# Output projection of an attention layer by token halves, with the values of a head in two runs and a third bank for transposes

## The chip, the cores and the metric

The kernel runs on one core of a Trainium2 chip. A core has TensorE (matmuls, with results in the banks of PSUM), VectorE, ScalarE and GpSimd, which here hardly works, and SyncE (SP), which issues the transfers from HBM. The profile calls them PE, DVE, ACT, POOL and SP. What is measured is the device time of one launch in microseconds; the time of a kernel is the median of several runs.

## The reference, cut to what matters

Two layers work on 512 latent tokens with 1024 features and 256 context tokens. Each layer is a feed-forward block, a mixer and a second feed-forward block; the mixer of layer 0 is a gated convolution, that of layer 1 is attention with 8 heads of queries, two of keys and values and a head size of 128. All data are fp32. The change touches the attention, the residual behind it and the start of the norm of the last feed-forward block:

```python
def gqa_block(q, k, v):
    s = jnp.einsum('bqkgd,bskd->bkgqs', q, k).astype(jnp.float32) * (HEAD_DIM ** -0.5)
    p = jax.nn.softmax(s, axis=-1).astype(v.dtype)
    return jnp.einsum('bkgqs,bskd->bqkgd', p, v)
...
    y_lat = o_l @ w_o                              # attention_mixer, o_l: (1, 512, 8 * 128)
...
        x_lat = x_lat + m_lat[:, 1, 2] * y_lat     # reference, layer 1
        h = norm_modulate(x_lat, norm_g[i, 2], m_lat[:, 2, 0], m_lat[:, 2, 1])
        x_lat = x_lat + MACARON_WEIGHT * m_lat[:, 2, 2] * swiglu(h, ffn_w_in[i, 1], ffn_w_out[i, 1])
```

Keys and values cover 768 tokens, context and latent; in layer 1 only the 512 latent tokens have queries and an output. `norm_modulate` needs the sum of the squares of all 1024 features of a token, so the norm of a token can begin only when its whole projection is done.

## The kernel before

**Products.** Features lie on the partitions (8 chunks m of 128), tokens in the columns. Every fp32 operand is split in two fp32r parts, high and low: ScalarE copies the high part (L184), VectorE subtracts it and writes the low part (L185). A product is then three matmuls, high by high, high by low and low by high (`mm3`, L805 to L807). A split of a weight tile of 128x512 is thus one instruction on each of the two engines, and so is every operand that TensorE is to read.

**Weights.** `w_list` lists all weight tiles in the order of their use, each with a place and, if its place comes free late, an event that must have been passed before the split may be written. `w_fill(k)` issues up to k further splits from this list at the point of the program where it stands, `w_get(k)` takes the next tile, and fills as far as k allows before, `w_done()` gives back the places of the tiles taken (`GRANULES` is their number). SP issues the raw transfers well ahead, in the order of the list.

**Order.** TensorE and SP execute in program order. The instructions of ScalarE and VectorE are put in order by a list scheduler when the kernel is built, which may pull a split or a subtract ahead of what stands before it in the program; between `in_order()` and `free_order()` they stay as written.

**Scores.** 8 heads by 4 blocks of 128 tokens are 32 blocks, n = 0 to 31. `scores` makes 6 matmuls into a tile of ps_C (two banks; there are two such tiles), then the max (VectorE, L1435), its product with the scale of the queries (L1436), the exponential with its sum on ScalarE (L1438), the reciprocal of the sum (L1439), and the scaling of the row, on ScalarE in odd blocks (L1441), on VectorE in even ones (L1443). `turn` transposes the 768 columns of the block in two half-turns of three (L1454), each into one of the two T banks, and splits each. `values` multiplies two blocks at once with the values: 18 matmuls of 256 columns into ps_O, whose result is split into o. In the loop the scores run two blocks ahead, and the values of a pair run behind the turn of the next block: scores(n+2), turn(n), then for even n values. A pair below is two scores, two turns, one run of values.

Ahead of the loop stand the value projections, `value_chunk` 0 to 5 (24 matmuls into ps_B, results read out by L1386 and L1387), and between them the norms of the last queries; chunks 4 and 5 stand behind the first two scores.

**Output projection.** While heads 4 to 7 run, a filler (`out_steps`, L856 on) does the part of heads 0 to 3: per m one group of 12 matmuls (4 heads, three parts) with all 512 columns into the bank of ps_A, which is the bank S, and an eviction that adds the group to x (L871). Behind the loop `out_close` does heads 4 to 7, first for token half one (columns 0 to 255), then for half two, 12 matmuls of 256 columns per m and half, evictions at L941. Its weight tiles 0 to 5 are held in slots that come free with the event "heads", at the end of the loop, so they are split there; the two others lie in homes wo0 and wo1.

**The norm of the last block.** For a token half: "squares" per m (ScalarE L594, VectorE L595), "parts" splits the sum (th on ScalarE L614, tl on VectorE L615), "root" adds over the partitions with two matmuls (L621, L622) and takes the root, and "normed", "modulated" and "parted" make the operands of the last feed-forward block. In `out_close` root of half one stands behind the second group of the second pass; that of half two stands in the opening of the feed-forward block. That block opens with steps of 24 matmuls (four times 6, 256 columns each), and `OPENING` says behind which six of them each part of the norm is put: key (2, 1) is step 2, behind its second six.

Of the kernel before, what the change touches and what calls it, by code (L numbers as in the profile page):

```python
# [41 lines left out]
HALF = D // 2  # L42
CONV_PARTS = (4, 4)
# [30 lines left out]
HELD_AFTER_HEADS = ((4, 5), (8, 9))  # L74
# [51 lines left out]
def backbone(ctx: ExitStack, tc: tile.TileContext, a: dict, out: bass.AP):  # L126
# [108 lines left out]
    def place(n, where, k):  # L235
# [5 lines left out]
        elif where[0] == "home":  # L241
            t = homes[where[1]](f"w{n}")
        else:
# [148 lines left out]

    def w_list():
# [573 lines left out]

    OPENING = {(0, 0): [("squares", 1, [7])], (0, 2): [("parts", 1)], (2, 0): [("root", 1)],
# [7 lines left out]
    def opening_hooks(op, count):  # L976
# [6 lines left out]
        hooks = {at: do(items) for at, items in OPENING.items()}  # L983
# [273 lines left out]
    def attention(gp, i, s, after):  # L1257
# [8 lines left out]
        for u in range(2):  # L1266
            homes["o", u] = lambda n, u=u: gp.tile([P, 2, D // 2], F32R, name=n, tag=f"wo{u}")
        part_tiles[:] = (gp, "th"), (gp, "tl")

        with psum(B=2, S=1, Q=1), ExitStack() as core:  # L1270
# [102 lines left out]
            def value_chunk(sc):  # L1373
                post = heads.pop(0)() if heads else None
                p = ptile("B", (P, 2, 256))[:, 0, :]
                ts = slice(sc * P, (sc + 1) * P)
                for k in range(KC):
                    if post and k == KC // 2:
                        post()
                    wvh, wvl = (t[:, 2 * (k % 2) : 2 * (k % 2) + 2, :] for t in wv[k // 2])  # L1380
# [3 lines left out]
                for g in range(KVH):  # L1384
                    pg = p[:, g * HD : (g + 1) * HD]
                    act.activation(vh[g][:, sc, :], pg, AF.Copy)  # L1386
                    dve.tensor_tensor(out=vl[g][:, sc, :], in0=pg, in1=vh[g][:, sc, :].bitcast(F32), op=ALU.subtract)  # L1387
# [14 lines left out]
            dve.tensor_scalar_mul(nrq, nrq, -isq)  # L1402

# [13 lines left out]
            st = {}  # L1417
# [28 lines left out]
            def turn(h, blk, pr):  # L1446
# [4 lines left out]
                for c0 in (0, 3):  # L1451
                    pt = ptile("T", (P, 4, P))[:, :3, :]
# [6 lines left out]
            def values(h, half, ph, pl):  # L1459
                g = h // 4  # L1460
                if half == 0:
                    st["po"] = ptile("O", (P, 2, 2 * P))
                    if h % 4 == 0:
                        st["o"] = o_tiles(g)
                p = st["po"][:, half, :]
                for c in range(6):
                    mm3(p, vh[g][:, c, :], vl[g][:, c, :], ph[:, c, :], pl[:, c, :], c == 0, c == 5)
                hs = slice(half * 2 * P, (half + 1) * 2 * P)
                oh, ol = st["o"]
                split(oh[h % 4][:, hs], ol[h % 4][:, hs], p)  # L1470

# [314 lines left out]
```

## Time and profile before

| | us |
|---|---|
| median of 3 runs | 2434.13 |
| lowest and highest | 2431.51, 2436.7 |
| the profiled execution, whole | 2436.43 |
| its span in the trace | 2434.7 |

| stretch of the span, us | length | TensorE busy | VectorE busy | ScalarE busy |
|---|---|---|---|---|
| 0 to 1850, all up to the attention | 1850 | 1832.2 | 1536.4 | 810.0 |
| 1850 to 1914, keys, queries, values | 64 | 62.68 | 54.21 | 42.86 |
| 1914 to 2053, scores and output projection | 139 | 130.22 | 107.23 | 97.13 |
| 2053 to 2110, second pass and opening | 57 | 54.55 | 43.37 | 35.67 |
| 2110 to 2434.7, last feed-forward block | 324.7 | 315.68 | 249.66 | 163.47 |

The busy time of TensorE counts a matmul from its start to its modelled end, also when it runs at a lower clock; so a stretch in which TensorE is busy throughout can still lose time, and the granted clock has to be read beside it. In rows of the profile L12 is line 12 of the kernel, `ps_T<-ident,pr` is an instruction that writes ps_T and reads ident and pr, `x3` is a count, and `[0.34 <-DVE p L185]` says that the engine stood for 0.34 us ahead of the row and what released it. In rows of the timeline the first number is the time from the start of the span and the second a duration, both in us.

### The profile page before, as it was taken

The page shows a single profiled execution, that of the slowest core. Times are in us where ns is not written, and L with a number is a line of the kernel's source. Part 1 is how long each engine was busy: PE and PEld are TensorE (multiplying, and loading weights), DVE is VectorE, ACT ScalarE, POOL GpSimd, SP SyncE. Part 2 cuts the span into 40 slices and gives each one's busy share as a digit, 9 for nine tenths or more (in the row PEclk, how much of TensorE's full clock was granted, in tenths as well). Part 3 has the DMA queues.
Part 4 walks back from the last instruction along what each step waited for, and adds up shares of the span by engine and source line. Part 5 has one row for each costly group of instructions (what it writes and reads, how often), then busy time and mean ns, then how long its engine had stood idle before and what let it go on. Part 6 is the DMA issues. An engine that isn't in the chain of part 4 may idle for free.

```text
span 2434.7 us, 37332 instructions
## 1 busy us (share of the span) xinstructions
PE 2395.3 (98%) x14316; PEld 2265.7 (93%) x14316; DVE 1990.9 (82%) x3979; ACT 1149.1 (47%) x2174; POOL 1.2 (0%) x8
## 2 busy tenths in 40 slices
PE   7999999999999999999999999999999999999998
PEld 4999999999999999999999999999997888899998
DVE  5789889878989898888887978778778787787776
ACT  4443343355535643443445534334346676555555
POOL 0000000000000000000000000000000000000000
PEclk9999999999999999999999999999999999999999
DMA  8243433430433033423331234324432102133332
GB/s 279 95 147 117 148 113 117 139 121 18 123 98 113 22 98 129 130 88 120 128 108 46 87 106 159 126 87 147 135 113 70 36 1 68 56 103 105 104 100 65
DMA packets 109411, 253.68 MB, mean 104 GB/s; under 512 B 10288, under 2 KB 19632, under 8 KB 109232
## 3 DMA queue, kind: packets, MB, share of 16 engines
q1 hardware_dynamic: 108384, 250.12, 31.9%
q8 instruction: 112, 1.84, 0.3%
q10 hardware_dynamic: 848, 1.18, 0.1%
q14 instruction: 67, 0.55, 0.1%
HBM read 249.16 MB, written 2.10 MB: 103 GB/s over the span
## 4 chain that ended last, share of the span: by engine, by line
PE 89%; DVE 5%; ACT 3%; DMA 2%; issue 1%; SPq 0%; DVEq 0%; ACTq 0%
PE ps_A L805 15%; PE ps_A L806 15%; PE ps_A L807 15%; PE ps_C L805 11%; PE ps_C L806 11%; PE ps_C L807 11%; PE ps_B L807 3%; PE ps_B L806 2%; PE ps_B L805 2%; DVE w L185 1%; ACT pr L1438 1%; PE ps_T L1454 1%; DMA ada<-in_ada_w 0%; DVE f L738 0%; DVE sm L1435 0%
## 5 line engine op out<-in xcount | busy, mean ns | idle before, releaser
L184 ACT ACTIVATE w<-raw 128x512 fp32r<-128x512 f32 (+2 forms) x865 | 519.5, 618 | 683.9 <-PE ps_A L807 200.0
L185 DVE TENSOR_TENSOR w<-raw,w 128x512 fp32r<-128x512 f32 (+2 forms) x865 | 572.7, 677 | 111.0 <-ACT w L184 103.2
L352 DVE TENSOR_TENSOR raw<-raw,raw 128x512 f32<-128x512 f32 x261 | 179.0, 688 | 27.3 <-DMA raw<-in_ffn_w_in 23.5
L805 PE MATMUL ps_C<-gh,w 128*128 128x512 f32 (+1 forms) x544 | 193.4, 355 | 1.7 <-DVE g L1091 1.6
L806 PE MATMUL ps_C<-gl,w 128*128 128x512 f32 (+1 forms) x544 | 193.4, 356 | 0.0
L807 PE MATMUL ps_C<-gh,w 128*128 128x512 f32 (+1 forms) x544 | 193.0, 355 | 0.0
L807 PE MATMUL ps_A<-gh,w 128*128 128x256 f32 (+1 forms) x544 | 180.6, 332 | 0.0
L806 PE MATMUL ps_A<-gl,w 128*128 128x256 f32 (+1 forms) x544 | 180.5, 332 | 0.0
L805 PE MATMUL ps_A<-gh,w 128*128 128x256 f32 (+1 forms) x544 | 180.3, 331 | 0.0
L871 DVE SCALAR_TENSOR_TENSOR x<-ps_C,gat,x 128x512 f32<-128x512 f32 (+1 forms) x156 | 102.7, 658 | 87.4 <-PE ps_C L807 87.2
L805 PE MATMUL ps_A<-tB11h,w 128*128 128x384 f32 (+1 forms) x400 | 130.5, 326 | 2.2 <-ACT tB11h L760 2.2
L806 PE MATMUL ps_A<-tB11l,w 128*128 128x384 f32 (+1 forms) x400 | 130.0, 325 | 0.3 <-DVE tB11l L762 0.3
L807 PE MATMUL ps_A<-tB11h,w 128*128 128x384 f32 (+1 forms) x400 | 129.9, 325 | 0.0
L806 PE MATMUL ps_C<-tB22l,w 128*128 128x384 f32 (+1 forms) x380 | 122.7, 323 | 0.0
L807 PE MATMUL ps_C<-tB22h,w 128*128 128x384 f32 (+1 forms) x380 | 122.7, 323 | 0.0
L805 PE MATMUL ps_C<-tB22h,w 128*128 128x384 f32 (+1 forms) x380 | 122.7, 323 | 0.0
L871 DVE SCALAR_TENSOR_TENSOR x<-ps_A,gat,x 128x512 f32<-128x512 f32 (+1 forms) x164 | 100.1, 611 | 24.4 <-PE ps_A L807 23.7
L805 PEld LDWEIGHTS ps_C<-gh,w 128*128 128x128 f32 x544 | 103.0, 189 | 16.4 <-ACT cy L1197 1.7
L807 PEld LDWEIGHTS ps_C<-gh,w 128*128 128x128 f32 x544 | 102.8, 189 | 14.6
L806 PEld LDWEIGHTS ps_C<-gl,w 128*128 128x128 f32 x544 | 103.0, 189 | 12.8
L805 PEld LDWEIGHTS ps_A<-gh,w 128*128 128x128 f32 x544 | 103.2, 190 | 11.2
L806 PEld LDWEIGHTS ps_A<-gl,w 128*128 128x128 f32 x544 | 103.2, 190 | 11.1
(410 smaller groups left out, 6888.9 us busy)
## 6 DMA issues: line engine op xcount, KB each, us to landing
raw<-in_ffn_w_in SPq DMA_DIRECT2D x170, 512.0 KB, 4.1
aw<-in_ada_t SPq DMA_DIRECT2D x240, 256.0 KB, 2.7
raw<-in_ffn_w_out SPq DMA_DIRECT2D x76, 512.0 KB, 4.4
raw<-in_conv_w_in SPq DMA_DIRECT2D x24, 512.0 KB, 3.6
ada<-in_ada_w SPq DMA_DIRECT2D x27, 256.0 KB, 5.4
raw<-in_attn_w_qkv SPq DMA_DIRECT2D x12, 512.0 KB, 4.4
raw<-in_ada_w SPq DMA_DIRECT2D x8, 512.0 KB, 4.5
crow<-in_c_rows SPq DMA_DIRECT2D x8, 512.0 KB, 5.5
```

What stands on the lines that cost most here:

```text
L184: act.activation(dsth, src, AF.Copy)
L185: dve.tensor_tensor(out=dstl, in0=src, in1=dsth.bitcast(F32), op=ALU.subtract)
L352: dve.tensor_tensor(out=quad(o), in0=quad(x), in1=quad(y), op=ALU.subtract)
L805: pe.matmul(ps, wh, xh, start=first, stop=False, **kw)
L806: pe.matmul(ps, wh, xl, start=False, stop=False, **kw)
L807: pe.matmul(ps, wl, xh, start=False, stop=last, **kw)
L871: dve.scalar_tensor_tensor(out=x, in0=p[:, o - off : o - off + w], scalar=gat[:, m, v : v + 1], in1=x, op0=ALU.mult, op1=ALU.add)
L1438: act.activation(pr, sc, AF.Exp, bias=sm[:, 1:2], scale=rq[:, blk, h : h + 1], accum_out=sm[:, 2:3])
L1454: pe.transpose(pt[:, c, :], pr[:, (c0 + c) * P : (c0 + c + 1) * P], ident)
```

## The change

The projection of heads 0 to 3 among the scores now covers only token half one; half two is projected behind the loop over all 8 heads at once. In detail:

- *Filler.* `out_steps` is no longer used here. In odd blocks from n = 17 on, `add_first(m)` issues one group of 12 matmuls with 256 columns for half one and heads 0 to 3, and keeps the weight tile.
- *Close.* `attention_close` takes the place of `out_close`: a first pass for half one over heads 4 to 7 (12 matmuls per m), a second for half two over all heads (24 per m). Root of half one stands behind the first group of the second pass. One split for the last feed-forward block stands in the first pass (behind m = 1) and one behind each group of the second; the preload of ScalarE's table is gone from it.
- *Values.* `values` is a generator that gives control back after 9 of its 18 matmuls; the second run of 9 comes behind the next turn.
- *Third bank.* For heads 0 to 3 every third half-turn writes to bank S in place of T.
- *Weights of the projection.* `o_place` puts tiles 4 to 7 of the first four heads behind the event "late" (n = 4), the first four tiles of the others into homes (wo0, wo1, and the freed places of keys and values of group 0), three into the slots 9 and 10 behind "turned" (n = 27) and the last into th, tl behind "heads". `FILLS` lists the blocks in which one split is asked for.
- *Start.* The value chunks are put in another order with the rest of the queries' norm: chunk 3 stands behind the transposes and the root.
- *Opening.* `LAST_MOVED` puts the parts of the norm of half two, from its root on, one step (24 matmuls) earlier. It is used for the last block alone.

SP issues the same transfers in the same order.

```diff
+FILLS = (6, 9, 12, 15, 18, 20, 22, 24, 27, 28, 29)
-HELD_AFTER_HEADS = ((4, 5), (8, 9))
+HELD_AFTER_HEADS = (9, 10)
...
+    def o_place(g, m):
+        if g == 0:
+            return None, "late" if m >= 4 else None
+        if m < 4:
+            return ("home", ("o", m)), "late"
+        if m < 7:
+            return ("oheld", HELD_AFTER_HEADS, m - 4), "turned"
+        return ("home", ("o", 4)), "heads"
...
-        add_out(a["attn_w_o"], 0, 4)
-        last_two = iter((0, 1))
-        add_out(a["attn_w_o"], 4, 4, HELD_AFTER_HEADS, "oheld", ("heads", "heads"), lambda: ("home", ("o", next(last_two))))
+        for g in range(2):
+            for m in range(0, KC, 2):
+                n = raw_add(a["attn_w_o"][:, m : m + 2, 4 * g : 4 * g + 4, :], (2, 4), 2)
+                for u in range(2):
+                    add_plain(n, u, slice(0, 4), *o_place(g, m + u))
...
+    def attention_close(old, new, units, op):
+        one, two = lay["tokens"]
+        behind = {0: [("root", 0), ("normed", 0, 0, 0), ("squares", 1, [0])], 1: [("modulated", 0, 0, 0), ("normed", 0, 0, 1), ("parted", 0, 0, 0, "hi"), ("squares", 1, [1])],
...
+        in_order()
+        fresh = []
+        for m in range(KC):
+            fresh.append(w_get(0))
+            add_heads(one, m, [(fresh[m], new)], out_banks(one, 1)[0])
+            op["squares"](0, [m])
+            if m == 1:
+                w_fill(1)
+        op["parts"](0)
+        op["start"]()
+        for m in range(KC):
+            unit, where = units[m]
+            add_heads(two, m, [(unit, old), (fresh[m], new)], out_banks(two, 1)[0])
+            taken.extend(where)
+            w_done()
+            for name, *args in behind.get(m, ()):
+                op[name](*args)
+            w_fill(1)
+        held_tiles.clear()
+
+    def add_heads(grp, m, sources, ps):
+        off, n = grp
+        todo = [(*unit, oh[f], ol[f], f) for unit, (oh, ol) in sources for f in range(4)]
+        for q, (wh, wl, xh, xl, f) in enumerate(todo):
+            mm3(ps[:, :n], wh[:, f, :], wl[:, f, :], xh[:, off : off + n], xl[:, off : off + n], q == 0, q == len(todo) - 1)
...
+        dve.scalar_tensor_tensor(out=x, in0=ps[:, :n], scalar=gat[:, m, 0:1], in1=x, op0=ALU.mult, op1=ALU.add)
...
+    LAST_MOVED = {(2, 0): (1, 0), (2, 1): (1, 1), (2, 2): (1, 2), (2, 3): (1, 3), (3, 0): (2, 0), (3, 1): (2, 1)}
...
-            for sc in range(3):
-                value_chunk(sc)
+            value_chunk(0, 2)
+            value_chunk(1, 1)
+            assert not heads
             sums = tmp.tile([P, NL], F32, name="r8", tag="r", bufs=2)
             act.activation(sums, pq, AF.Copy)
-            value_chunk(3)
+            value_chunk(2)
...
+            value_chunk(3)
...
-                    pt = ptile("T", (P, 4, P))[:, :3, :]
+                    st["turns"] += 1
+                    pt = ptile("T" if h >= 4 or st["turns"] % 3 else "S", (P, 4, P))[:, :3, :]
...
                 for c in range(6):
                     mm3(p, vh[g][:, c, :], vl[g][:, c, :], ph[:, c, :], pl[:, c, :], c == 0, c == 5)
+                    if c == 2:
+                        yield
...
+            def add_first(m):
+                mark = len(taken)
+                unit = w_get(0)
+                units.append((unit, taken[mark:]))
+                del taken[mark:]
+                add_heads(HALVES[0], m, [(unit, st["o", 0])], ptile("A"))
...
+                if n == 4:
+                    traced.add("late")
+                if n == 27:
+                    traced.add("turned")
+                if n == 16:
+                    bank["A"] = bank["S"]
+                if n in FILLS:
+                    w_fill(1)
                 p = turn(h, blk, ready[n])
                 ready[n] = None
-                if late:
-                    values(*late)
-                    if late[:2] == (3, 1):
-                        bank["A"] = bank["S"]
-                        filler = out_steps(((0, NL),), None, *st["o"], 4, None, banks, 1)
-                    late = None
-                elif n > 16:
-                    next(filler, None)
+                next(work, None)
                 if blk % 2:
-                    late = (h, blk // 2, *p)
+                    work = values(h, blk // 2, *p)
+                    if n > 16:
+                        add_first((n - 17) // 2)
...
-            ffn(gp, 1, 2, "final", None, opening_hooks(op4, 12), LAST_PARTS, last_order, LAST_DIRECT)
+            ffn(gp, 1, 2, "final", None, opening_hooks(op4, 12, LAST_MOVED), LAST_PARTS, last_order, LAST_DIRECT)
```

What this moves on the engines that hand work to TensorE, at three places. First VectorE in the middle of heads 0 to 3, about one pair of blocks; L1435 (now L1500) is the max, L1436 (L1501) its product, L1439 (L1504) the reciprocal of the sum, L1443 (L1508) the scaling of an even block, and L185 (L186) with p the subtract of a half-turn, with o that of the values. Before:

```order
L1435 TENSOR_REDUCE sm<-ps_C 128x1
L1439 RECIPROCAL sm<-sm 128x1
L185 TENSOR_TENSOR p_18816<-ps_T,p_18815 128x3x128
L1436 TENSOR_TENSOR sm<-sm,nrq 128x1
L185 TENSOR_TENSOR p_18816<-ps_T,p_18815 128x3x128
L1439 RECIPROCAL sm<-sm 128x1
L1443 TENSOR_SCALAR pr<-pr,sm 128x768
L185 TENSOR_TENSOR o_18600<-ps_O,o_18599 128x256
L1435 TENSOR_REDUCE sm<-ps_C 128x1
L185 TENSOR_TENSOR p_18816<-ps_T,p_18815 128x3x128
L1436 TENSOR_TENSOR sm<-sm,nrq 128x1
L185 TENSOR_TENSOR p_18816<-ps_T,p_18815 128x3x128
```

With the change:

```order
L1500 TENSOR_REDUCE sm<-ps_C 128x1
L1504 RECIPROCAL sm<-sm 128x1
L186 TENSOR_TENSOR p_18819<-ps_T,p_18818 128x3x128
L1501 TENSOR_TENSOR sm<-sm,nrq 128x1
L186 TENSOR_TENSOR p_18819<-ps_S,p_18818 128x3x128
L1500 TENSOR_REDUCE sm<-ps_C 128x1
L1504 RECIPROCAL sm<-sm 128x1
L186 TENSOR_TENSOR p_18819<-ps_T,p_18818 128x3x128
L1508 TENSOR_SCALAR pr<-pr,sm 128x768
L1501 TENSOR_TENSOR sm<-sm,nrq 128x1
L186 TENSOR_TENSOR p_18819<-ps_T,p_18818 128x3x128
L186 TENSOR_TENSOR o_18600<-ps_O,o_18599 128x256
```

Between the product L1501 and the next reciprocal L1504 there now stand a subtract and the next max, where one subtract alone stood before; one subtract in three reads bank S, and the subtract of o stands behind both subtracts of a turn.

Second VectorE at the end of the first pass of the close; L595 (L610) adds the squares, L941 (L1022) is the eviction of a group, L615 (L630) makes tl, w<-raw is the split of a weight for the next block. Before:

```order
L595 TENSOR_TENSOR ssq<-ssq,sq 128x256 x3
L185 TENSOR_TENSOR w_20006<-raw_19872,w_20006 128x512
L185 TENSOR_TENSOR w_20009<-raw_19878,w_20009 128x512
L185 TENSOR_TENSOR w_20012<-raw_19872,w_20012 128x512
L185 TENSOR_TENSOR w_20017<-raw_19878,w_20017 128x512
L941 SCALAR_TENSOR_TENSOR x<-ps_C,gat,x 128x256
L941 SCALAR_TENSOR_TENSOR x<-ps_A,gat,x 128x256
L595 TENSOR_TENSOR ssq<-ssq,sq 128x256 x2
L615 SCALAR_TENSOR_TENSOR tl<-ssq,eps_76,th 128x256
```

With the change:

```order
L1022 SCALAR_TENSOR_TENSOR x<-ps_C,gat,x 128x256
L610 TENSOR_TENSOR ssq<-ssq,sq 128x256
L1022 SCALAR_TENSOR_TENSOR x<-ps_A,gat,x 128x256
L610 TENSOR_TENSOR ssq<-ssq,sq 128x256
L630 SCALAR_TENSOR_TENSOR tl<-ssq,eps_76,th 128x256
L642 SCALAR_TENSOR_TENSOR scl<-mods_81,packed 128x8
L1022 SCALAR_TENSOR_TENSOR x<-ps_C,gat,x 128x256
L620 TENSOR_TENSOR r<-y 128x256
L621 SCALAR_TENSOR_TENSOR r<-ps_S,r 128x256
L622 SCALAR_TENSOR_TENSOR r<-r,y 128x256
L753 TENSOR_TENSOR f_20068<-x,r 128x512
L186 TENSOR_TENSOR w_20071<-raw_19098,w_20071 128x512
```

The four splits are gone from the place ahead of the last two evictions; evictions and sums alternate, tl follows at once, and the root (L620 to L622) stands behind one eviction of the second pass.

Third ScalarE at the start of the scores; L1438 (L1503) is the exponential, L1441 (L1506) the scaling of an odd block, L1386 (L1447) reads out a value chunk, w, p, qh and oheld are copies of high parts (w and oheld of weights). Before:

```order
L184 ACTIVATE w_19181<-raw_18038 128x512
L184 ACTIVATE w_19184<-raw_18038 128x512
L184 ACTIVATE w_19189<-raw_18086 128x512
L1438 ACTIVATE pr,sm<-ps_C,sm,rq 128x768
L1386 ACTIVATE vh_17664<-ps_B 128x128
L184 ACTIVATE w_19192<-raw_18086 128x512
L1441 ACTIVATE pr<-pr,sm 128x768
L184 ACTIVATE p_18526<-ps_T 128x3x128
L1386 ACTIVATE vh_17665<-ps_B 128x128
L1438 ACTIVATE pr,sm<-ps_C,sm,rq 128x768
```

With the change:

```order
L1503 ACTIVATE pr,sm<-ps_C,sm,rq 128x768
L185 ACTIVATE w_18855<-raw_18038 128x512
L1506 ACTIVATE pr<-pr,sm 128x768
L1447 ACTIVATE vh_17664<-ps_B 128x128
L185 ACTIVATE w_18976<-raw_18086 128x512
L1447 ACTIVATE vh_17665<-ps_B 128x128
L185 ACTIVATE p_18526<-ps_T 128x3x128
L185 ACTIVATE w_19095<-raw_18086 128x512
L185 ACTIVATE oheld_19651<-raw_18253 128x512 x2
L1503 ACTIVATE pr,sm<-ps_C,sm,rq 128x768
L185 ACTIVATE p_18526<-ps_T 128x3x128
L185 ACTIVATE p_18526<-ps_S 128x3x128
```

The copies of w stay at this place, now behind the exponential, and two copies of oheld stand ahead of the exponential that followed the read-out before.

More of the change, by code (lines that the diff above doesn't have):

```diff
@@ L242, in place @@
             t = homes[where[1]](f"w{n}")
+            if isinstance(t, list):
+                return [z[:, : k * P].rearrange("p (k c) -> p k c", c=P) for z in t]
         else:
@@ L982, in do @@
             return go
-        hooks = {at: do(items) for at, items in OPENING.items()}
+        hooks = {moved.get(at, at): do(items) for at, items in OPENING.items()}
         if count > 8:
@@ L1267, in attention @@
             homes["o", u] = lambda n, u=u: gp.tile([P, 2, D // 2], F32R, name=n, tag=f"wo{u}")
+        for u, tags in ((2, ("kh0", "kl0")), (3, ("vh0", "vl0")), (4, ("th", "tl"))):
+            homes["o", u] = lambda n, tags=tags: [gp.tile([P, D // 2], F32R, name=f"{n}{t}", tag=t) for t in tags]
         part_tiles[:] = (gp, "th"), (gp, "tl")
@@ L1371, in attention, with value_chunk @@
             wv = [w_get() for _ in range(4)]
-            def value_chunk(sc):
-                post = heads.pop(0)() if heads else None
+            def value_chunk(sc, count=0):
+                post = heads.pop(0)() if count else None
                 p = ptile("B", (P, 2, 256))[:, 0, :]
@@ L1379, in value_chunk @@
                         post()
+                        post = heads.pop(0)() if count > 1 else None
                     wvh, wvl = (t[:, 2 * (k % 2) : 2 * (k % 2) + 2, :] for t in wv[k // 2])
@@ L1416, in attention @@
             gates.append(lambda: gate_vec(i, s, False))
-            st = {}
+            st = {"turns": 0}
             def scores(h, blk):
@@ L1477, in attention @@
             w_done()
-            late = None
-            filler = iter(())
+            work = iter(())
             for n, (h, blk) in enumerate(blocks):
@@ L1482, in attention @@
                     ready.append(scores(*blocks[n + 2]))
+                if n == 4:
[6 more added lines that the diff above has]
+                    w_fill(1)
                 p = turn(h, blk, ready[n])
                 ready[n] = None
-                if late:
-                    values(*late)
-                    if late[:2] == (3, 1):
-                        bank["A"] = bank["S"]
-                        filler = out_steps(((0, NL),), None, *st["o"], 4, None, banks, 1)
-                    late = None
-                elif n > 16:
-                    next(filler, None)
+                next(work, None)
                 if blk % 2:
-                    late = (h, blk // 2, *p)
-            values(*late)
-            for _ in filler:
+                    work = values(h, blk // 2, *p)
+                    if n > 16:
+                        add_first((n - 17) // 2)
+            for _ in work:
                 pass
-            oh, ol = st["o"]
             traced.add("heads")
@@ L1503, in attention @@
         stage["banks"].enter_context(psum(A=3, B=1, C=3, S=1))
-        out_close(oh, ol, 4, after)
+        attention_close(st["o", 0], st["o", 1], units, after)
     def out_last(gh, gl, npart, gp):
```

16 lines of the change are left out of this document (13 added, 3 removed).

## The prediction

> **What bounds the kernel now.** I read the page first: its span, its engine rows and its chain.
>
> ```profile
> span 2434.7 us, 37332 instructions
> PE 2395.3 (98%) x14316; PEld 2265.7 (93%) x14316; DVE 1990.9 (82%) x3979; ACT 1149.1 (47%) x2174; POOL 1.2 (0%) x8
> PE 89%; DVE 5%; ACT 3%; DMA 2%; issue 1%; SPq 0%; DVEq 0%; ACTq 0%
> ```
>
> TensorE holds 89% of the chain, so the change can win only where TensorE stands still or runs slowly inside the code it touches: attention, the projection behind it and the start of the last feed-forward layer. Next comes a table of windows over that part. Its columns are the stretch, its length, then busy time and count for PE, PEld, DVE, ACT and POOL, the granted clock, the DMA share and GB/s.
>
> ```profile
> 1914.00:1932.00 18.00, 14.90 (x87) 12.98 (x86) 13.67 (x33) 12.51 (x26) 0.00 (x0) 0.81 0.19 58
> 1932.00:1970.00 38.00, 35.99 (x255) 31.86 (x254) 31.63 (x76) 30.40 (x64) 0.00 (x0) 1.00 0.01 1
> 1970.00:2032.00 62.00, 62.00 (x409) 56.58 (x408) 44.98 (x99) 40.51 (x80) 0.00 (x0) 1.00 0.00 1
> 2032.00:2053.00 21.00, 17.33 (x142) 17.00 (x140) 16.96 (x33) 13.71 (x27) 0.00 (x0) 0.99 0.55 175
> 2053.00:2065.00 12.00, 11.81 (x74) 11.58 (x75) 9.28 (x21) 8.34 (x19) 0.00 (x0) 0.74 0.10 34
> 2065.00:2093.00 28.00, 25.74 (x204) 24.62 (x203) 19.41 (x40) 16.58 (x34) 0.00 (x0) 1.00 0.00 1
> 2093.00:2110.00 17.00, 17.00 (x123) 16.64 (x122) 14.68 (x29) 10.76 (x25) 0.00 (x0) 0.90 0.43 124
> ```
>
> The rows are: start of the scores, heads 0 to 3, heads 4 to 7 with the old filler, the old close (two rows), the opening of the last layer (two rows). In three of them the clock is below 1. One minus the clock, times the length, is work time lost: 0.19 x 18 = 3.4, 0.26 x 12 = 3.1, 0.10 x 17 = 1.7 us. Then the waits of TensorE between 1906 and 2110 (total, times, longest):
>
> ```profile
> PE ps_T L1454 <- DVE p L185: 4.5, 6, 2.1
> PE ps_S L621 <- ACT th L614: 3.9, 1, 3.9
> PE ps_C L807 <- DVE w L185: 1.8, 1, 1.8
> ```
>
> Transposes wait for VectorE to empty the two T banks; the root of the close waits for the sum of squares; a weight of the last layer is split too late. These waits (10.2) and the clock (8.2) together are 18.4 us, and shorter delays, as in heads 0 to 3 below, come on top. This is the pool from which the change can draw.
>
> **TensorE's own work.** The projection of heads 0 to 3 ran as 8 groups of 12 matmuls with 512 columns; it becomes 16 groups with 256, eight among the scores and eight in the close.
>
> ```profile
> 2023.56 0.48 PE L805 MATMUL ps_A<-o,w 128*128 128x512 f32 x1
> ...
> 2026.38 0.82 PE L1454 MATMUL ps_T<-ident,pr 128*128 128x128 f32 x6
> ```
>
> ```profile
> 2041.97 0.28 PE L805 MATMUL ps_A<-o,oheld 128*128 128x256 f32 x1
> ...
> 2043.41 0.28 PE L805 MATMUL ps_C<-o,w 128*128 128x256 f32 x1
> ```
>
> Twelve take 2.82 us at 512 and 1.44 at 256. So 8 x 2.82 = 22.6 becomes 16 x 1.44 = 23.0: +0.5 us, and up to +1.3 if each extra group's first matmul starts late, as those behind transposes do (here 2023.56 to 2023.87). I take **+1.0**. The Trainium skill ("TensorE: Matmul & The Clock Gate", Back-to-back issue gap) gives a warm gap of N/2.4 + 2.5 ns, 216 ns at 512 and 109 at 256; by it the split would cost an estimated 0.25 us. The rows here, 0.235 and 0.120 us per matmul, decide.
>
> **Heads 0 to 3** (-3.4). A pair of blocks is two scores, two turns and one run of values.
>
> ```profile
> 1937.61 1.08 PE L1454 MATMUL ps_T<-ident,pr 128*128 128x128 f32 x6 [0.34 <-DVE p L185]
> 1943.92 1.08 PE L1454 MATMUL ps_T<-ident,pr 128*128 128x128 f32 x6 [0.34 <-DVE sm L1436]
> 1981.59 0.82 PE L1454 MATMUL ps_T<-ident,pr 128*128 128x128 f32 x6
> 1989.87 0.82 PE L1454 MATMUL ps_T<-ident,pr 128*128 128x128 f32 x6
> ```
>
> The pair takes 6.31 us in heads 0 to 3 and 8.28 in heads 4 to 7, where TensorE never waits (62.00 busy of 62.00). Take the filler off: 8.28 - 2.82 = 5.46 us is a pair's own work, so 0.85 us per pair stands still, over 38 / 6.31 = 6 pairs 5.1 us. Two views say why:
>
> ```profile
> 1932.00:1938.30 6.30, 5.96 (x43) 5.28 (x43) 4.99 (x13) 5.29 (x12) 0.00 (x0) 1.00 0.01 3
> 1938.30:1944.60 6.30, 5.96 (x43) 5.27 (x43) 5.49 (x14) 4.78 (x11) 0.00 (x0) 1.00 0.00 1
> ```
>
> ```profile
> DVE sm L1439 <- ACT pr L1438: 5.6, 6, 1.1
> ```
>
> VectorE is busy 4.99 and 5.49 us of a pair, and idles 5.6 / 6 = 0.93 us because its reciprocal stands right behind the max of the same block, with the exponential still running. In the changed order (first piece of the section on the change) a subtract and the next max stand between, so this wait should go; the third bank lets the first transposes of a turn start while VectorE holds T, and the values come in two runs of nine, so the next scores start about 1 us earlier. Then VectorE needs some 5.25 us a pair, ScalarE 5.0, TensorE 5.46. Three engines this close will not all be met; I take 5.75 us, gain 0.56 x 6. Bounds: 1 and 5.
>
> **Start of the scores** (-2.5).
>
> ```profile
> 1914.67 1.28 DVE L185 TENSOR_TENSOR w<-raw,w 128x512 fp32r<-128x512 f32 x2
> ...
> 1918.44 0.28 DVE L1387 TENSOR_TENSOR vl<-ps_B,vh 128x128 fp32r<-128x128 f32 x1
> ```
>
> The second half-turn waited 2.1 us for a T bank, because three of the four remaining weight splits and a max stood before the last value chunk was read out at 1918.44. Behind that the clock fell. The new code asks for those splits later (FILLS), but the scheduler still places all four here, now two of them behind the first subtract, and pulls three ScalarE copies (oheld) up to this place. I count about 1 us sooner release of the bank, about half of the first run of values no longer in front of scores, and some relief of the 3.4 us of clock: 2.5 us. Bounds: 0 (the copies block ScalarE) and 5. The page named above (What's actually happening) says that the clock falls after an idle window of about 3.4 us; here it fell behind a wait of 2.1 us and, at 2093, behind one of 1.8, so shorter waits than the page's matter and the trace disagrees with it.
>
> **Heads 4 to 7** (+1.2).
>
> ```profile
> 2025.88 0.16 DVE L1439 RECIPROCAL sm<-sm 128x1 f32<-128x1 f32 x1 [0.74 <-ACT pr L1438]
> ```
>
> TensorE needs 5.46 + 1.44 = 6.90 us per pair. VectorE has 5.25, the eviction of 256 columns and in four pairs a split of a weight, which used to stand in the close (0.4 and 0.6 us, from the 0.48 and from 2.50 / 4 of the next part's rows); one reciprocal still waits for its exponential, about as in the row. That is 5.25 + 0.4 + 0.6 + 0.74, with shorter waits 7.2 in four pairs, 0.3 over TensorE: 4 x 0.3 = 1.2. The eviction waits for TensorE's twelve matmuls, and behind it stands the next max. Bounds: 0, if the max comes later anyway; 4, if each pair loses 0.5.
>
> **The close** (-6.5).
>
> ```profile
> 2046.25 1.28 ACT L598 ACT_TABLE_LOAD   x1
> ...
> 2052.63 0.51 ACT L614 ACTIVATE th<-ssq,eps 128x256 fp32r<-128x256 f32 x1 [0.63 <-DVE ssq L595]
> ```
>
> ```profile
> 2048.21 2.50 DVE L185 TENSOR_TENSOR w<-raw,w 128x512 fp32r<-128x512 f32 x4 [1.09 <-ACT w L184]
> 2050.62 0.48 DVE L941 SCALAR_TENSOR_TENSOR x<-ps_C,gat,x 128x256 f32<-128x256 f32 x1
> ...
> 2051.64 0.95 DVE L595 TENSOR_TENSOR ssq<-ssq,sq 128x256 f32<-128x256 f32 x2 [0.15 <-ACT sq L594]
> ```
>
> The last evictions of the first token half came at 2050.62, behind a table load and four splits for the next layer; so th came at 2052.63, TensorE stood 3.86 us and then lost 3.1 us of clock. Now only one split stands in the first pass, there is no table load in it, and root stands behind one group of 24 matmuls (2 x 1.44 = 2.88 us). The chain from the last matmul is eviction 0.48, square and sum 0.9 (the sum is half of 0.95, the square much alike), th 0.51, tl about as long, with handoffs some 2.7 us: just covered. If this cover fails by 0.3 it costs 0.3. The eight splits now follow one after each group of the second pass: the old second pass had VectorE busy 9.28 and ScalarE 8.34 of 12.00 us, and eight splits of 0.62 make 14.2 and some 13 of the new pass's 8 x 2.88 = 23. I leave 0.5 of the 7.0 us in place. Bounds: 4 and 7. SP issues the same transfers in the same order.
>
> **The opening** (-4.0).
>
> ```profile
> 2072.85 0.43 DVE L605 TENSOR_TENSOR r<-y 128x256 f32<-128x256 f32 x1 [2.88 <-ACT y L604]
> ...
> 2091.82 0.68 DVE L185 TENSOR_TENSOR w<-raw,w 128x512 fp32r<-128x512 f32 x1
> ```
>
> VectorE idled 2.88 us for the second root, then had hardly a break until the late split at 2091.82 for which TensorE waited 1.8 us. LAST_MOVED puts the root one step (24 matmuls, 2.88 us) earlier, into that idle time. The stage holds 28.00 - 25.74 = 2.3 us idle, late starts of single matmuls that the view counts as busy, by my estimate 1.5, and 1.7 of clock, together 5.5; I keep 1.5 of it. Bounds: 1 and 5.5.
>
> **Sum.** +1.0 - 2.5 - 3.4 + 1.2 - 6.5 - 4.0 = -14.2 us. The profiled execution took 2436.4 us, 2.3 above the median of the three, so it would become 2422.2, and the median 2434.1 - 14.2 = **2420 us**.
>
> **Rivals.** (1) *The start stays as it is*: the scheduler leaves the splits there, ScalarE gets more, the clock falls again. For it: the four splits did not move away. Its price is the 2.5: 2422.5, and with half of the gain in heads 0 to 3 gone too **2424**. (2) *VectorE becomes the bound of the scores*: every pair of heads 4 to 7 costs 7.7 instead of 6.90 and heads 0 to 3 stay at 6.1. 8 x 0.8 = 6.4 in place of 1.2, and 1.3 in place of 3.4: +7.3, 2427. Against it: in the old stage VectorE was busy 44.98 of 62.00 us, 6.0 a pair, and it now has a smaller eviction. (3) *The change does not do what it says*: the halves are projected, but the root still waits. Then close and opening gain 3 instead of 10.5: 2427.5. (4) *Slower*: the second pass of the close becomes bound by VectorE and ScalarE, which hand work to each other four times per group. Past 2.88 us per group it delays the second root; at 5.0 us it costs 8 x 2.1 = 17 us, and the clock 3.4: 2420 + 20 = 2440. Against it: 14.2 busy of 23 us. (5) *All covers hold*: 2413.
>
> **How the numbers follow.** Forecast 0.60, rival 1 0.14, rival 2 0.09, rival 3 0.06, rival 4 0.06, rival 5 0.05. A measurement of this kernel tells about 0.2%, 4.9 us, from no change: under 2429.3 is faster, over 2439.0 slower. Rivals 2 and 3 spill about half beyond 2429.3. Faster 0.60 + 0.14 + 0.05 + 0.08 = 0.87, same 0.07, slower 0.06. The bounds all low add up to about -1, all high to -22; I leave out a tenth at each end: 2413 to 2428.
>
> **What would show it.** Right: between scores and close no wait of TensorE over 1.5 us; pairs of 5.6 to 5.9 and then 6.9 to 7.3 us; L636, the new line of root's first matmul, without a wait in the close and a granted clock of 1.00 there; no 1.8 us wait for w in the opening. Wrong: a clock below 1 in the stretch of heads 0 to 7, waits of TensorE for DVE p that do not shrink, or a root that still waits 3 us behind the first pass.

## The result and the profile after

| | before | changed |
|---|---|---|
| median, us | 2434.1 (2431.51 to 2436.7, 4 runs) | 2416.9 (2416.08 to 2417.69, 4 runs) |
| ratio | | 0.9929 (95% interval 0.9912 to 0.9947) |
| profiled execution, its span | 2436.43, 2434.7 | 2417.69, 2415.9 |

The change takes 17.2 us off, where 14.2 were forecast, and 2416.9 lies in the range of 2413 to 2428. The page of the changed kernel, its span, its engines and its chain:

```profile
span 2415.9 us, 37519 instructions
...
PE 2385.5 (99%) x14412; PEld 2262.9 (94%) x14412; DVE 1987.6 (82%) x3979; ACT 1146.6 (47%) x2173; POOL 1.2 (0%) x8
...
PE 92%; DVE 4%; ACT 2%; DMA 1%; issue 1%; SPq 0%; DVEq 0%; ACTq 0%
```

The windows of the changed kernel, in the order of those of before: start of the scores, heads 0 to 3, heads 4 to 7, first pass of the close, second pass, opening. Busy time and count stand there for PE, PEld, DVE, ACT and POOL, then the granted clock, the DMA share and GB/s.

```profile
1905.40:1921.70 16.30, 14.77 (x108) 13.45 (x107) 12.55 (x30) 12.55 (x29) 0.00 (x0) 1.00 0.22 65
1921.70:1955.60 33.90, 33.76 (x254) 31.77 (x253) 31.58 (x77) 31.77 (x66) 0.00 (x0) 1.00 0.01 1
1955.60:2014.00 58.40, 58.33 (x454) 56.02 (x454) 48.99 (x115) 43.60 (x87) 0.00 (x0) 1.00 0.06 19
2014.00:2026.30 12.30, 12.30 (x104) 12.30 (x104) 6.19 (x14) 3.77 (x9) 0.00 (x0) 1.00 0.15 45
2026.30:2050.00 23.70, 23.70 (x200) 23.70 (x199) 18.06 (x37) 15.05 (x32) 0.00 (x0) 1.00 0.14 45
2050.00:2100.00 50.00, 48.54 (x359) 46.16 (x359) 37.56 (x72) 27.89 (x57) 0.00 (x0) 1.00 0.25 75
```

The clock is 1.00 in every row, and TensorE is busy almost throughout from heads 0 to 3 to the end of the close (33.76 of 33.90 us in the row with the most left). The waits of TensorE from 1900 to 2100, with total, times and longest, are 2.9 us in place of the 10.2 and more of before:

```profile
PE ps_T L1520 <- DVE sm L1501: 1.5, 2, 1.2
PE ps_C L822 <- DVE w L186: 1.0, 2, 0.6
PE ps_C L820 <- ACT w L185: 0.4, 1, 0.4
```

The wait for th in the close is gone, and that for p. Rows of the timeline from the close show by how much the root of half one is covered:

```profile
2028.21 0.51 ACT L629 ACTIVATE th<-ssq,eps 128x256 fp32r<-128x256 f32 x1 [0.49 <-DVE ssq L610]
2028.75 0.48 DVE L630 SCALAR_TENSOR_TENSOR tl<-ssq,eps,th 128x256 fp32r<-128x256 f32 x1 [0.58 <-ACT th L629]
...
2029.30 0.28 PE L636 MATMUL ps_S<-th,ones_r 128*128 128x256 f32 x1
2029.42 0.28 PE L637 MATMUL ps_S<-tl,ones_r 128*128 128x256 f32 x1
```

tl ends at 2029.23 and the matmul that reads it starts at 2029.42: the group of 24 matmuls covers the chain with 0.19 us to spare.

**Losses by stage.** For the comparison of all runs I add up, over each stage, what lies between the starts of two neighbouring matmuls beyond the usual spacing (0.227 us for 512 columns, 0.173 for 384, 0.119 for 256, 0.095 for a transpose). That holds waits, single late starts and a lower clock alike. The stages end with the third score matmul of block 4, the third of block 17, the values of the last pair, the matmul ahead of the root of half two (which stands in the opening of the feed-forward block) and 59 us behind the root of half one; what lies ahead of a matmul counts for the stage of this matmul. The last column but one is the time from the start of the first score to the end of the span, which leaves out what the part ahead of the attention does from run to run: the first score started between 1903.3 and 1907.5 us, with no order among the kernels. All but the last column come from one execution each. (The medians stem from several sets of runs; that of the kernel before lay between 2433.0 and 2434.5 in them. One of the six runs of full_rows took 3368.94 us at a granted clock of 0.653 and is left out of its median.) Halved clock: the time, from the start of the span, and its length.

| kernel | start | heads 0-3 | heads 4-7 | close | opening | clock halved between 1900 and 2400 | first score to end | median |
|---|---|---|---|---|---|---|---|---|
| before | 5.45 | 6.59 | 2.54 | 7.16 | 5.59 | 1919.4 for 6.8, 2052.5 for 6.8, 2093.5 for 3.4 | 527.7 | 2434.1 |
| before_again | 4.20 | 5.57 | 2.54 | 5.88 | 5.44 | 2050.7 for 3.4 | 523.5 | |
| before_third | 4.18 | 5.55 | 2.54 | 6.12 | 5.45 | 2049.8 for 3.4 | 523.7 | |
| changed | 1.81 | 2.58 | 2.23 | 0.28 | 2.56 | none | 510.5 | 2416.9 |
| two_banks | 3.19 | 2.49 | 2.22 | 0.28 | 2.56 | none | 511.7 | 2418.26 |
| one_run | 1.81 | 5.03 | 2.71 | 0.28 | 2.56 | none | 513.4 | 2420.82 |
| old_start | 2.78 | 2.41 | 2.24 | 0.28 | 2.54 | none | 511.2 | 2419.06 |
| scores_old | 5.43 | 6.60 | 2.64 | 0.28 | 2.55 | 1919.1 for 6.8 | 518.4 | 2425.01 |
| not_moved | 1.83 | 2.56 | 2.23 | 0.28 | 5.60 | 2076.4 for 3.4 | 513.5 | 2419.86 |
| full_rows | 1.82 | 2.57 | 1.93 | 1.59 | 9.73 | 2057.5 for 6.8 | 517.6 | 2426.19 |
| root_first | 1.82 | 2.57 | 2.23 | 4.60 | 2.58 | 2030.8 for 3.4 | 514.8 | 2421.73 |
| before_moved | 4.20 | 5.57 | 2.55 | 7.24 | 3.92 | 2048.6 for 6.8 | 523.5 | 2432.14 |
| both | 1.15 | 4.31 | 2.23 | 0.28 | 0.34 | none | 509.3 | 2416.78 |
| early_fill | 1.83 | 2.55 | 2.23 | 0.28 | 0.34 | none | 508.2 | 2415.99 |

Against the first profile of before the stages gain 3.6, 4.0, 0.3, 6.9 and 3.0 us, 17.9 together, and another 0.4 comes behind them. TensorE's own work in the finer groups takes 1.1 of it back (192 matmuls of 0.119 us in place of 96 of 0.227). That makes 17.2 net, as the times from the first score to the end say, 527.7 and 510.5.

### The profile page after: what moved, and what is told of

It is laid out like the page before. It is cut to its first block, busy times and chain, and to the rows that moved or that the text cites. A ratio compares the mean times of both kernels' runs of the same rounds, so it can differ in the third digit from the quotient of the medians.

```text
span 2415.9 us, 37519 instructions
## 1 busy us (share of the span) xinstructions
PE 2385.5 (99%) x14412; PEld 2262.9 (94%) x14412; DVE 1987.6 (82%) x3979; ACT 1146.6 (47%) x2173; POOL 1.2 (0%) x8
## 4 chain that ended last, share of the span: by engine, by line
PE 92%; DVE 4%; ACT 2%; DMA 1%; issue 1%; SPq 0%; DVEq 0%; ACTq 0%
PE ps_A L820 16%; PE ps_A L821 16%; PE ps_A L822 16%; PE ps_C L820 11%; PE ps_C L821 11%; PE ps_C L822 11%; PE ps_B L822 3%; PE ps_B L821 3%; PE ps_B L820 3%; PE ps_T L1520 1%; DMA ada<-in_ada_w 0%; DVE f L753 0%; PE ps_O L820 0%; PE ps_O L821 0%; PE ps_O L822 0%
## 5 line engine op out<-in xcount | busy, mean ns | idle before, releaser
L185 ACT ACTIVATE w<-raw 128x512 fp32r<-128x512 f32 (+2 forms) x865 | 519.9, 618 | 689.2 <-PE ps_A L822 197.5
L186 DVE TENSOR_TENSOR w<-raw,w 128x512 fp32r<-128x512 f32 (+2 forms) x865 | 574.2, 678 | 106.5 <-ACT w L185 97.6
L822 PE MATMUL ps_B<-tB21h,w 128*128 128x384 f32 (+1 forms) x348 | 112.6, 323 | 0.3 <-DVE w L186 0.3
```

What stands on the lines that cost most here:

```text
L185: act.activation(dsth, src, AF.Copy)
L186: dve.tensor_tensor(out=dstl, in0=src, in1=dsth.bitcast(F32), op=ALU.subtract)
L822: pe.matmul(ps, wl, xh, start=False, stop=last, **kw)
```

## The experiments

**Which part carries the scores.** Four kernels take parts of the change back, all else left as it is.

`two_banks`:

```diff
-                    pt = ptile("T" if h >= 4 or st["turns"] % 3 else "S", (P, 4, P))[:, :3, :]
+                    pt = ptile("T", (P, 4, P))[:, :3, :]
```

> All half-turns go to the two T banks. Theory 'third bank': the pairs of heads 0 to 3, 5.56 us with the change and 6.31 before, go back to 6.0 or more and TensorE waits for DVE p again; the time is 3 to 5 us above the changed kernel. Rival 'two runs': a bank is free again because nine matmuls (1.1 us) stand between two turns' ends and the next scores; pairs stay at 5.56 to 5.65 and the time rises by less than 1 us.

`one_run`, where the generator now never yields:

```diff
-                    if c == 2:
+                    if c > 5:
                         yield
```

> The 18 matmuls of the values come in one run again, third bank and all else kept. Theory 'two runs': pairs of heads 0 to 3 go back to 5.9 to 6.3 us, since two scores and two turns follow each other without cover and the reciprocal stands right behind the product of its block again; +3 to +5 us, in heads 4 to 7 up to 2 more. Rival 'third bank': pairs stay below 5.7, time within 1 us of the changed kernel.

`old_start`:

```diff
-            value_chunk(0, 2)
-            value_chunk(1, 1)
-            assert not heads
+            value_chunk(0, 1)
+            value_chunk(1, 1)
+            value_chunk(2, 1)
...
-            value_chunk(2)
+            value_chunk(3)
...
-            value_chunk(3)
```

> Only the order of the value chunks and of the last queries' norm is that of before. Theory: the start lost 7.2 us before and 2.6 with the change, and the chunk order is a small part of it: +0 to +1.5 us, clock at 1.00. Rival: the early root of the queries is what lets the first exponential start in time; then the wait of 2 us at the first turns and the half clock come back and the time rises by 3 to 5 us.

`scores_old`: the three edits together.

> Two banks, one run and the old chunk order together; the halves, the close, the late fills and the moved root stay. If these three parts carry start and heads 0 to 3, both stages go back to what they lost before: 7 us (with the half clock) and 6 us, +8 to +9 us above the changed kernel. If the later splits (FILLS) carry part of it, the start loses less than 7 and the sum is +4 to +6.

The waits of TensorE from 1903 to 2015 with two banks:

```profile
PE ps_T L1520 <- DVE p L186: 1.3, 1, 1.3
PE ps_T L1520 <- DVE sm L1501: 1.2, 1, 1.2
```

and with the values in one run:

```profile
PE ps_T L1520 <- DVE sm L1501: 1.9, 3, 1.2
PE ps_T L1520 <- DVE p L186: 1.0, 3, 0.5
PE ps_S L1520 <- DVE p L186: 0.3, 1, 0.3
```

With two banks there is a single additional wait of 1.3 us in these lists, at the start. Heads 0 to 3 lose 2.49 us as against 2.58, but this sum hides a part: in the two blocks right behind the start two_banks loses 0.2 and the changed kernel 1.1, and from block 6 to block 16 two_banks loses 1.8 and the changed kernel 1.0. Rows of two_banks, the first score of every second block:

```profile
1927.80 0.40 PE L1496 MATMUL ps_C<-kh,qh 128*128 128x512 f32 x1
...
1933.75 0.40 PE L1496 MATMUL ps_C<-kh,qh 128*128 128x512 f32 x1
...
1939.30 0.40 PE L1496 MATMUL ps_C<-kh,qh 128*128 128x512 f32 x1
...
1945.27 0.40 PE L1496 MATMUL ps_C<-kh,qh 128*128 128x512 f32 x1
```

Every second pair takes 5.95 or 5.97 us in place of 5.56. So the third bank saves 1.3 us at the start, of which 0.9 comes back in the next two blocks, and 0.8 later, in delays that are too short for the list of waits.

With the values in one run the start is unchanged and heads 0 to 3 lose 5.03, 2.45 more, mostly in half-turns that start up to 0.5 us late. VectorE's wait for the exponential, 5.6 us in the kernel before, is back with it. Here are the longest waits of VectorE over the same blocks, first in one_run (1924 to 1953), then with the change (1926 to 1955), where it waits for scores instead:

```profile
DVE sm L1504 <- ACT pr L1503: 3.8, 5, 1.0
DVE sm L1500 <- PE ps_C L1498: 2.3, 4, 0.8
```

From block 6 to block 16, where no clock was halved, the loss is 1.0 us with the change, 1.8 in two_banks, 3.4 in one_run, 4.4 in scores_old and 4.5 in before_again. So there the values in two runs carry 2.4 to 2.6 and the third bank 0.8 to 1.0.

The old chunk order alone costs 1.0 at the start. The wait there is 2.1 us in place of 1.2, with the clock at 1.00:

```profile
PE ps_T L1519 <- DVE p L186: 2.1, 1, 2.1
```

The medians of the three stand 1.4, 3.9 and 2.2 us above the changed kernel; only in one_run does every single run lie above all of the changed kernel, so for the other two it is the traces that show the loss. The three together bring start and heads 0 to 3 back to 5.43 and 6.60, what the first profile of before shows (5.45 and 6.59), with the clock halved at the same place, so that the later requests for splits (FILLS) and the event "late" carry nothing there. Alone they cost 1.3 + 2.45 + 0.8 = 4.5 in these two stages, together 7.6. Of the difference of 3.1 about 2.3 goes with the halved clock, which came in none of the three alone: that much more the first profile of before loses in these stages than before_again (12.0 against 9.8).

**Which part carries close and opening.**

`not_moved`:

```diff
-            ffn(gp, 1, 2, "final", None, opening_hooks(op4, 12, LAST_MOVED), LAST_PARTS, last_order, LAST_DIRECT)
+            ffn(gp, 1, 2, "final", None, opening_hooks(op4, 12), LAST_PARTS, last_order, LAST_DIRECT)
```

> Without LAST_MOVED, all else as changed. By the trace the opening (from the close to 59 us behind the root of half one) lost 5.6 us before and 2.6 with the change. Theory: the earlier root is that gain; +2.5 to +3.5 us, the wait for a late w split is back at 1.5 to 2 us. Rival: the gain came from the close, which hands over sooner; +0 to +1 us.

`full_rows`, where heads 0 to 3 are projected for all 512 tokens among the scores; the output is complete:

```diff
-                add_heads(HALVES[0], m, [(unit, st["o", 0])], ptile("A"))
+                add_heads((0, NL), m, [(unit, st["o", 0])], ptile("A"))
...
-            add_heads(two, m, [(unit, old), (fresh[m], new)], out_banks(two, 1)[0])
+            add_heads(two, m, [(fresh[m], new)], out_banks(two, 1)[0])
```

> The filler does all 512 columns for heads 0 to 3 again, and the second pass only heads 4 to 7, 12 matmuls per group; the places of weights, the splits and all else stay as changed. Theory 'cover': root of half one then has 1.44 us of cover in place of 2.88 and waits about 1.2 us, and the second pass of 11.5 us has 18 us of VectorE work, so the opening waits 4 to 7 us for the norm, and the clock may fall: +4 to +10 us. Rival 'splits': the gain of the close came from taking splits and the table load out of the first pass, not from the halves: within 1.5 us of the changed kernel.

`root_first`:

```diff
-        behind = {0: [("root", 0), ("normed", 0, 0, 0), ("squares", 1, [0])], 1: [("modulated", 0, 0, 0), ("normed", 0, 0, 1), ("parted", 0, 0, 0, "hi"), ("squares", 1, [1])],
+        behind = {0: [("normed", 0, 0, 0), ("squares", 1, [0])], 1: [("modulated", 0, 0, 0), ("normed", 0, 0, 1), ("parted", 0, 0, 0, "hi"), ("squares", 1, [1])],
...
         op["start"]()
+        op["root"](0)
```

> Root of half one stands ahead of the second pass, with no matmuls to cover it. Theory: TensorE waits for eviction, square, sum and th, about 2.5 us; the clock falls behind it as it did behind waits of 2.1 and 1.8 us before, costing up to 3.4 us more: +2.5 to +6 us. Rival on the clock: a wait alone does not lower it, +2 to +2.6 us with the clock at 1.00.

`before_moved`: the kernel before, with LAST_MOVED and the two edits in `opening_hooks` that it needs.

> The kernel before with LAST_MOVED alone. Theory: the earlier root fills VectorE's idle time there as well, 2 to 4 us below before. Rival: with the old close half one is not ready a step earlier, so root of half two only takes a place in front of it, and the time stays within 1 us of before.

The waits of TensorE for the norm with full rows (2026 to 2100), and the root of half two in its timeline:

```profile
PE ps_S L636 <- ACT th L629: 7.0, 2, 6.3
```

```profile
2061.01 0.58 PE L636 MATMUL ps_S<-th,ones_r 128*128 128x256 f32 x1 [6.30 <-ACT th L629]
```

Its close has no splits of the next block ahead of the last evictions and no table load, and the root of half one waits only 0.7 us; but the second pass, shorter by 8 x 12 matmuls, no longer holds the work of VectorE and ScalarE. It falls behind, and the root of half two waits 6.3 us. Close and opening lose 11.3 in place of 2.8 us. So, with splits and roots placed as in the change, the token halves carry this gain: the matmuls that they move behind the loop are the cover of the norm. That the kernel before loses a like sum, 12.75, has another cause, its wait of 3.9 us at the first root, and 3.1 of this wait went without the halves. Full rows with the root of half two at its old, later place were not run, so what the halves are worth beside that remedy is not shown. The time is 9.3 us above the changed kernel by the medians, 7.1 from the first score on.

Without LAST_MOVED the late split is back, and the clock falls behind it:

```profile
PE ps_C L822 <- DVE w L186: 1.8, 1, 1.8
```

The opening loses 5.60 in place of 2.56 and the time rises by 3.0 us, as the first theory had it. In the kernel before the same edit takes the loss of the opening from 5.44 (before_again) to 3.92, 1.5 us, but its clock in the close was halved for 6.8 us and not for 3.4, and from the first score to the end both take 523.5. Its ratio, 0.9993 (0.9985 to 1.0002), does not tell it from no change; the 2 to 4 us of the theory did not come. There two splits are late all the same:

```profile
PE ps_C L807 <- DVE w L185: 1.0, 2, 0.6
PE ps_S L621 <- ACT th L614: 0.7, 1, 0.7
```

The second row is a new wait: half two's root, one step earlier, is now too early for its sum.

With the root first TensorE waits 2.2 us for th and the clock is halved for 3.4 us: +4.3 us in the close, 4.8 by the medians.

```profile
PE ps_S L636 <- ACT th L629: 2.2, 1, 2.2
```

The group of 24 matmuls thus saves both.

**What is left.** `both`:

```diff
-            st = {"turns": 0}
+            st = {"turns": 1}
...
+                if k == 0 and half and key == "f12":
+                    w_fill(2)
                 if (n, k) in hooks:
```

> Two waits that the changed kernel still has are aimed at. The third bank is used one half-turn earlier (second, fifth, eighth half-turn), so that the second half-turn of the scores does not wait for the bank of the last value chunk (1.2 us); and in the opening of the last block two splits of weights are asked for at the start of a step, ahead of the sums, in place of one behind them (waits of 1.0 and 0.4 us). Theory: the start loses 0.6 in place of 1.8 us, the opening 1.0 in place of 2.6: 2.0 to 2.8 us below the changed kernel. Rival: the same splits and sums only change places and what is late is then T1 or an eviction; the start's second half-turn waits for the max instead: within 0.6 us.

`early_fill`: the second edit alone.

> The changed kernel with the earlier splits in the opening alone; the third bank stands as in the change. In the run with both edits the opening lost 0.34 in place of 2.56 us, and the shifted third bank gained 0.7 us at the start and lost 1.7 in heads 0 to 3. Theory: the edits do not touch each other, so start and heads 0 to 3 are as with the change (1.8 and 2.6), the opening 0.3, and the time 2.0 to 2.4 us below the changed kernel. Rival: what heads 0 to 3 lost belongs to the kernel's state at large and stays; then no more than 1 us.

The waits of TensorE from 1900 to 2100, of early_fill:

```profile
PE ps_T L1522 <- DVE sm L1503: 1.5, 2, 1.2
```

In both kernels the waits for w are gone and the opening loses 0.34 in place of 2.56 us. The shifted third bank gained 0.7 at the start and lost 1.7 in heads 0 to 3, so `both` gave most of it back. From the first score to the end early_fill takes 508.2 us as against 510.5, the 2.3 that were expected, but its median, 2415.99 (2415.26 to 2417.55), lies only 0.9 below that of the change, and the runs overlap. The trace shows the gain; the whole time, with a part ahead of the attention that varies by up to 4 us, does not establish it.

**The clock.** `before_again` and `before_third` are the kernel before, unchanged.

> The kernel before once more, for its clock alone. In ten traces the granted clock changes only at times 3.413 us apart, a raster that lies differently in every execution, and it is halved in the piece behind one in which TensorE stood still 1.92 us or more, never behind 1.82 or less. Theory 'raster': the wait of 2.1 us at the start and that of 1.8 us in the opening halve the clock only if one piece of the raster holds 1.9 us of them, so they may do it here or not, and the wait of 3.9 us in the close always does. Rival 'wait': each wait that halved the clock in the first profile does it again.

> The same once more. Raster: as above, each of the two short waits is followed by a halved clock where a piece of the raster holds 1.9 us of standing still, and not otherwise; the close always. Rival: all three as in the first profile.

Windows of 3.41 us laid on the times at which the clock can change, TensorE alone, in the first profile of before:

```profile
1912.60:1916.01 3.41, 3.41 (x28) 1.00 0.00 0
1916.01:1919.42 3.41, 1.33 (x10) 1.00 0.62 175
1919.42:1922.83 3.41, 2.38 (x10) 0.50 0.37 132
```

and, with all engines, in before_again:

```profile
1914.19:1917.60 3.41, 2.30 (x17) 1.93 (x15) 3.29 (x9) 3.32 (x8) 0.00 (x0) 1.00 0.27 53
1917.60:1921.02 3.42, 1.94 (x12) 1.56 (x12) 1.92 (x4) 2.36 (x6) 0.00 (x0) 1.00 0.68 252
1921.02:1924.43 3.41, 2.59 (x20) 2.47 (x21) 3.25 (x10) 2.53 (x7) 0.00 (x0) 1.00 0.00 1
```

The same wait of 2.1 us (the longest in both traces) falls into one piece in the first, which stands still for 3.41 - 1.33 = 2.08 us, and the next runs at half clock; in the second it is cut in two, 1.11 and 1.48 with what follows, and the clock stays. Both later traces halved it in the close alone. The raster theory holds, that of the single wait does not.

## Why the prediction was right

- *TensorE's own work* (+1.0): 1.1 by the usual spacings.
- *Start* (-2.5): 3.6 against the first profile of before, 2.4 against the two whose clock did not fall there. The splits stayed where they were, as said, and the clock did not fall. The size was right for the waits, but the reasons were weighed otherwise than they measure: third bank 1.4 (0.9 of it comes back in the next two blocks), chunk order 1.0, values in two runs nothing here, and the relief of the clock was a matter of the execution.
- *Heads 0 to 3* (-3.4): 4.0, without the clock 3.0. These rows of the timeline, the first score of every second block, give the pair, 5.56 us in heads 0 to 3 and 7.00 in heads 4 to 7:

```profile
1938.56 0.40 PE L1496 MATMUL ps_C<-kh,qh 128*128 128x512 f32 x1
...
1944.12 0.40 PE L1496 MATMUL ps_C<-kh,qh 128*128 128x512 f32 x1
...
1986.43 0.40 PE L1496 MATMUL ps_C<-kh,qh 128*128 128x512 f32 x1
...
1993.43 0.40 PE L1496 MATMUL ps_C<-kh,qh 128*128 128x512 f32 x1
```

  The forecast of 5.75 allowed for three engines that are not all met; TensorE had hardly a wait left, so its own work, put at 5.46, is the pair. The wait of VectorE's reciprocal is gone, as forecast. Of the reasons the third bank is the small one, 0.8 us from block 6 to block 16, and the values in two runs carry 2.4 there. Their run of nine stands ahead of the next scores, and VectorE's order (the subtract and the next max ahead of the reciprocal) comes with it; the runs do not part these two.
- *Heads 4 to 7* (+1.2): -0.3. VectorE did not become late: 48.99 busy of 58.40 us, 5.9 us of a pair of 7.00 where 7.2 with its waits were forecast, and the reciprocal that waits for its exponential delays no matmul. This term had the wrong sign; the low bound, 0, was the nearest.
- *Close* (-6.5): 6.9, and 5.6 and 5.8 against the two later traces. Eviction, square, sum, th and tl were just covered, as worked out, and rival 4, the second pass bound by VectorE and ScalarE, did not come: 18.06 and 15.05 busy of 23.70 us, more than the 14.2 and some 13 of the forecast, but within the pass. It came in full_rows, where the pass is half as long.
- *Opening* (-4.0): 3.0, the term that was too large. The price of the clock, 1.7, was added to the waits. In before_again and before_third the clock stayed up in this stage, and it lost 5.44 and 5.45 nonetheless, as against 5.59 with the clock halved: while TensorE ran slowly the next splits were in time, and where it did not it waited for them. Before_again has these waits for w, where the first profile has the one of 1.8 alone:

```profile
PE ps_C L807 <- DVE w L185: 2.2, 2, 1.8
PE ps_C L805 <- ACT w L184: 0.4, 1, 0.4
```

  The clock loss stood in place of waits, not on top. The two splits that were still late with the change stand in the trace behind the sums, and asking for them earlier takes 2.2 us of the remaining 2.6.
- *The sum*: -14.2 in the forecast, -17.2 from the first score on, -17.2 by the medians. The 3.0 between them are 1.1 at the start, 0.6 in heads 0 to 3, 1.5 in heads 4 to 7, 0.4 in the close and 0.4 behind the opening, less 1.0 in the opening. In three stages the forecast counted the halved clock of one execution as the kernel's; only in the close does it come in each of the three traces of before, and there for 3.4 or 6.8 us. The three traces of before take 527.7, 523.5 and 523.7 us from the first score on, so about 4 us of such a difference are the position of the raster; against the two later traces the gain is 13.0 and 13.2 us. The granted clocks of whole runs tell how often that happens. Of 43 runs of before that were made beside the experiments nine had a clock of 0.998, as the two later traces, and a median of 2431.7 us; nine had 0.994, as the first profile, and 2436.0. The four runs of the changed kernel had 0.998 or 0.999. So at a like clock the gain is about 14.8 us, and some 2.4 of the 17.2 are halved clock that most runs of before have. That -14.2 lies so near to these figures is in part luck: measured against before_again the opening was put 1.1 and the close 0.9 too high, and the wrong sign in heads 4 to 7, worth 1.5, made up for most of it.

Of the signs, the root of half one without a wait, the clock of 1.00, no wait over 1.5 us and no wait of 1.8 for w all came; the pairs of 7.00 lie in their range, those of 5.56 just under it. None of the rivals came as a whole. Of rival 1 the condition came (the splits did not move) and not its consequence. Rival 5, that all covers hold, was nearest: but for 2.9 us of waits they held, and 2416.9 lies about midway between its 2413 and the 2420 of the forecast.

## What to carry to other kernels

When a norm or another chain between engines stands behind a projection, keep independent matmuls of that projection for this place, even if they could have run earlier as a filler: here the same matmuls hid nothing among the scores, where TensorE was busy in any case, and saved 7.1 us behind them (full_rows, from the first score on). And before a lower clock is priced into a change, look at a second execution: a wait near the limit halves the clock in one and not in the other, and some of what it costs would be a wait otherwise.

## What the runs showed of the clock

In the 14 traces of the table above, between 1000 and 2400 us, the granted clock changed only on a raster of 3.413 us, whose position differed from execution to execution. It was halved behind every piece in which TensorE stood still for 1.92 us or more (ten pieces, 1.92 to 3.41) and behind none with less; the largest of these was 1.82 us, in old_start. Where the halved piece itself had 0.54 us or more of standing still the next one was halved too, at 0.22 and less it was not. The Trainium skill ("TensorE: Matmul & The Clock Gate", What's actually happening) tells of a free-running window of 3413 ns, which the spacing bears out, and of a fall after an idle window; here a little over half a window without work was enough. So in the stretch looked at here a wait under 1.9 us cost its own length, one of 2.1 us by chance up to 3.4 more, and one of 3.9 us always more.

This border does not hold for all code. At the very end of the span, where few and small matmuls are left, the clock fell behind two pieces that stood still for less, 1.49 us in before and 1.54 in both. In before, TensorE alone:

```profile
2424.56:2427.98 3.42, 1.93 (x14) 1.00 0.40 147
2427.98:2431.39 3.41, 0.00 (x0) 0.50 0.85 290
```

What sets the border is open.
